# A hybrid trunk layer with a gated delta rule: token-major k, v and norms of q by VectorE's block transposes and copies between partitions

## The chip, the cores and the metric

The kernel runs on one core of one Trainium2 chip. The metric is the device time of one launch, in microseconds (us); the kernel before has a median of 2256.19 us over three runs, from 2256.06 to 2256.45.

A core has five engines that run their own instruction lists side by side: PE (matrix products), ACT (activations), DVE (element-wise work and reductions), POOL (a slower general engine) and SP, which here only issues DMAs. They meet at semaphores. SBUF is the on-chip memory of 128 partitions, PSUM the memory in which PE's products land.

## The reference

One decoder layer on 16 meta tokens and 2048 tokens with 1024 channels, all in float32:

```python
h = rmsnorm(x, norm_g); p = h @ w_in            # 1024 -> 8208 columns
q, k, v = split(silu(causal_dwconv4(p_qkv)))     # 8 heads of 128 channels
q = l2norm(q) * 128**-0.5;  k = l2norm(k)
g = -exp(A_log) * softplus(a + dt_bias);  beta = sigmoid(b)
o = chunk_gated_delta_rule(q, k, v, g, beta)     # state S per head, 128 x 128
#   S_t = a_t (I - beta_t k_t k_t^T) S_{t-1} + beta_t k_t v_t^T,   o_t = S_t^T q_t
o_dn = rmsnorm(o, dn_out_g) * silu(z_A)
o_sc = sc_b * causal_dwconv3(sc_c * sc_h) * silu(sc_z)
x = x + concat(o_dn, o_sc) @ w_out;  return rmsnorm(x, final_g)
```

The delta rule is worked out by chunks. Within a chunk a unit lower triangular matrix I + M is inverted, and from chunk to chunk only S is handed on. The sums of squares that normalize q are taken over a token's 128 channels, and the factor is applied to the output.

## The kernel before

The projection is the bulk of PE's work: 128 jobs, each 128 columns of `w_in` by the tokens of one half (1024 tokens, in three groups; the first half's first group holds the meta tokens too: 272, 384 and 384 tokens, 256 in the second half's first). Weights and activations are split into a high and a low part (`wh`, `wl`, `hh`, `hl`), so a group takes 24 matmuls: `mm<-hh,wh` and `mm<-hl,wh` in turn, then `mm<-hh,wl`. ACT takes a job's first tap of the convolution out of PSUM, DVE adds the other taps (rows `acc`). After both halves comes the output projection.

Beside the projections run four streams for 16 heads, 8 heads on each half, numbered 0 to 15 here. Each is a Python generator.

- `delta_front`: decays `E`, the products of k with k and of q with k, and the inverses of the 32 by 32 diagonal blocks. These are a chain of 31 pairs on DVE, `prod<-nb,XT` and `XT<-prod`. `prod` begins as a pattern copied from the constant `eyep`. Its result goes to `xtd` in DRAM in four copies.
- `delta_back`: four copies bring the blocks back as `W<-xtd`. k, v and q of a head lie channel-major, [channel, token]. PE transposes k (L1138), v (L1147) and q (L1158), 8 tiles of 128 by 128 each, in six batches of four; ACT writes k out of PSUM scaled into `kd`, DVE writes v times `ir` into `vr`, ACT squares q's transposes and accumulates the sums in `ssq`. The blocks are transposed (`X<-W`), and products p1 to p4 (`ta<-X,E` is p1) make the inverse of the whole chunk, in `W`. `qd<-ged` loads the decays, `qd<-qd,q` multiplies q by them.
- `delta_scan`: for each of 8 chunks of 128 tokens a chain over three engines: PE `rec<-S,k`, DVE `yy`, PE `rec<-yy,W`, ACT `vn`, PE `rec<-vn,kd`, DVE `S`; `o<-S,qd` and `o<-vn,P` give the output.
- `delta_out`: norm, gate and store.

The order on PE, ACT, DVE and POOL is what the program issues. Class `Model` (L30 to L107) keeps a planned clock for each engine and each tile; a stream yields the planned time until its next step can run, and between two projection pieces the streams that are due run their next step. A stream that isn't due leaves the place to projection matmuls. Where no projection piece may be issued yet, because a job is waiting for a stream (`require`), the planned clock is moved on and the streams' steps stand one behind the other. Requirements: the job of k of head i needs the scan of head i-2 done, q the blocks of head i-2, v the step ("vr", i-1), the gate's job the output of head i-2. `delta_back` of head i starts when `delta_front` of head i and the scan of head i-1 are through.

All DMAs are issued on SP, in the order in which the program gives them. Each signals on one of eight semaphores, taken in turn, and is issued only when the one eight places ahead has landed.

Of the kernel before, what the change touches and what calls it, by code (L numbers as in the profile page):

```python
# [29 lines left out]
class Model:  # L30
    """Time of each engine and of each tile, as work is issued; it decides the order of issue only."""
# [32 lines left out]
    def after(self, *aps, slot=None, eng=None, lag=0.0, least=0.02):  # L64
        """Time until the tiles are written, the slot is free and the engine is through but for lag."""
# [96 lines left out]
class Recorded:  # L162
    """The engines of a core, with all that they are given entered into the model."""
# [10 lines left out]
def hybrid_trunk(  # L174
# [41 lines left out]
    # ---- order of emission: a stream of projections, cut into pieces, and streams of dependent  # L216
    # steps that are issued between the pieces. `model` follows the engines as they are given work;
    # a step yields the time until what its successor needs is there.
# [28 lines left out]
    def when_done(fn, ap, most=100.0):  # L247
        """Issue fn once ap has been written."""
        timed.append((clk() + min(after(ap), most), fn))
# [46 lines left out]
    def newton(dst, a, y, t):  # L296
        """dst = y (1.5 - 0.5 a y^2): one Newton step for a ** -0.5 from y."""
        nc.vector.tensor_tensor(out=t, in0=y, in1=y, op=ALU.mult)
        nc.vector.scalar_tensor_tensor(t, t, -0.5, a, op0=ALU.mult, op1=ALU.mult)
        nc.vector.scalar_tensor_tensor(dst, t, 1.5, y, op0=ALU.add, op1=ALU.mult)  # L300
# [16 lines left out]
    # ---- constants of the first phase  # L317
# [12 lines left out]
    # eyep[32 q + block, m, i] = (i == 8 q + m)  # L330
    eyep = vt(pp, [128, 8, 32], "eyep")
# [10 lines left out]
    def constants():  # L342
# [29 lines left out]
        nc.gpsimd.memset(eyep, 0.0)  # L372
        for q in range(4):
            for m in range(8):
                nc.gpsimd.memset(eyep[32 * q : 32 * q + 32, m, 8 * q + m : 8 * q + m + 1], 1.0)
# [13 lines left out]
    def turn(hf, xt, k0, i, col, n, g):  # L389
        """Channels 4 k0 .. 4 k0 + 3 of a token tile into h^T."""  # L390
# [18 lines left out]
    def statistics(xt, n, jk):  # L409
        """mean square + eps and its approximate power -0.5."""  # L410
# [6 lines left out]
    def rootmean(xt, n):  # L417
        """(mean square + eps) ** -0.5 by ACT and GpSimd."""
# [14 lines left out]
    def prologue0():  # L433
        """h^T = (RMSNorm(x))^T of the first half as float32r parts hi + lo, [channel, k, token]
        by group."""
# [100 lines left out]
    def normalize(i):  # L536
        """RMSNorm of token tile i of the second half, to DRAM until the first half is through."""
        xt = vt(dp, [128, NC, 128], "kd").rearrange("p c i -> p (c i)")
        nc.sync.dma_start(xt, xs[HALF + 128 * i :][:128])
        yield after(xt)  # L540
        st = statistics(xt, 128, vt(dp, [128, 1840], "gw", dt=BF16))
# [48 lines left out]
    def hold(tag="ta", keep=False):  # L590
        """Wait until no step holds tag over several yields; or hold it."""
# [7 lines left out]
    def gates(hf):  # L599
        """Token-major gate values [128, head, chunk]; on half 0 chunk 8 holds the meta tokens."""  # L600
# [21 lines left out]
        gw = vt(dp, [128, 920], "gw")  # L622
# [24 lines left out]
        # e = exp(-|a|), exp(-|b|), exp(min(b, 0))  # L647
# [11 lines left out]
        # log1p(e) = 2 atanh(s), s = e / (2 + e) <= 1 / 3  # L659
# [35 lines left out]
        G[hf] = dict(beta=beta, gcum=gcum, neg=neg, nch=nch)  # L695
        yield 2.0
        done.add(("G", hf))

    # ---- projections
# [76 lines left out]
    def conv_job(hf, s, col, t, pre, emit):  # L776
        """Projection, causal width-4 convolution and SiLU of channel tile t of q | k | v."""
# [43 lines left out]
    def slot_jobs(hf, s):  # L821
# [51 lines left out]
        # short convolution of channel tile s  # L873
# [67 lines left out]
    # ---- gated delta rule  # L941
    def substitution(nb, XT, prod):
        """Rows of (I + N)^-1 of unit lower triangular 32 x 32 blocks, a block and 8 columns per
        partition; nb[j, i] = N[i, j], XT[col, i], prod[col, i] = identity on entry."""
# [9 lines left out]
    def decay(hf, row0, n, E, gc):  # L954
        """E[j, c, i] = exp(g_i - g_j) for i >= j, else 0."""
# [15 lines left out]
    def delta_front():  # L971
        """Decays, the two triangular matrices, and the inverses of the diagonal blocks."""
# [664 lines left out]
```

## Time and profile before

| | |
|---|---|
| median of three runs | 2256.19 us |
| span of the profiled execution | 2248.0 us |
| lies around it (difference) | 8.2 us |
| PE busy | 2175.4 us, 97% |
| DVE, ACT, POOL busy | 65%, 38%, 7% |

Busy time is the sum over an engine's instructions; what is not busy in the span is a wait. The profiled execution's own time is not recorded apart from its span, so the median stands for it: the two differ by 8.2 us, which are the launch and the end around the first and last instruction. Times in the rows are microseconds from the start of the span. Where a row says `x4`, four like instructions were put together; the start is that of the first.

### The profile page before, as it was taken

The page shows a single profiled execution, that of the slowest core. Times are in us where ns is not written, and L with a number is a line of the kernel's source. Part 1 is how long each engine was busy: PE and PEld are TensorE (multiplying, and loading weights), DVE is VectorE, ACT ScalarE, POOL GpSimd, SP SyncE. Part 2 cuts the span into 40 slices and gives each one's busy share as a digit, 9 for nine tenths or more (in the row PEclk, how much of TensorE's full clock was granted, in tenths as well). Part 3 has the DMA queues.
Part 4 walks back from the last instruction along what each step waited for, and adds up shares of the span by engine and source line. Part 5 has one row for each costly group of instructions (what it writes and reads, how often), then busy time and mean ns, then how long its engine had stood idle before and what let it go on. Part 6 is the DMA issues. An engine that isn't in the chain of part 4 may idle for free.

```text
span 2248.0 us, 38710 instructions
## 1 busy us (share of the span) xinstructions
PE 2175.4 (97%) x15024; PEld 2061.8 (92%) x15024; DVE 1456.6 (65%) x4031; ACT 864.9 (38%) x2080; POOL 153.3 (7%) x312
## 2 busy tenths in 40 slices
PE   6999999999999999999999999999998799999998
PEld 6999999999999998999999999999998798888886
DVE  4676867676767767776868677676766465544322
ACT  5534434444444333443434343525352324422111
POOL 4000100000000000101000000000000000000000
PEclk9999999999999999999999999999999899999999
DMA  6444345443535677524343544253546664645321
GB/s 140 75 81 70 84 68 91 67 93 67 92 67 104 82 83 60 134 43 80 52 83 57 78 52 83 48 88 43 88 49 60 53 94 139 222 164 189 119 94 57
DMA packets 257237, 196.46 MB, mean 87 GB/s; under 512 B 62085, under 2 KB 226446, under 8 KB 257054
## 3 DMA queue, kind: packets, MB, share of 16 engines
q1 hardware_dynamic: 257054, 194.00, 47.5%
q8 instruction: 118, 1.93, 0.4%
q14 instruction: 65, 0.53, 0.1%
HBM read 157.89 MB, written 36.06 MB: 86 GB/s over the span
## 4 chain that ended last, share of the span: by engine, by line
PE 87%; DMA 6%; DVE 4%; SPq 1%; ACT 1%; issue 1%; POOL 0%; POOLq 0%; DVEq 0%; ACTq 0%
PE mm L118 74%; PE ta L118 7%; PE rec L118 4%; PE o L118 2%; SPq L118 1%; DMA nb<-nbd 1%; DMA wr<-in_w_in_dram 1%; DMA kd<-in_x_dram 1%; DVE prod L118 1%; DMA xtd<-XT 1%; DMA W<-xtd 1%; ACT junk L118 1%; DVE acc L118 1%; DVE XT L118 1%; DMA nbd<-E 0%
## 5 line engine op out<-in xcount | busy, mean ns | idle before, releaser
L118 PE MATMUL mm<-hh,wh 128*128 128x384 f32 (+3 forms) x3328 | 1043.6, 335 | 6.4 <-ACT hh L118 5.3
L118 PE MATMUL mm<-hl,wh 128*128 128x384 f32 (+3 forms) x3328 | 1015.1, 326 | 0.0
L118 PEld LDWEIGHTS mm<-hh,wh 128*128 128x128 f32 x3328 | 626.8, 189 | 21.0 <-ACT hh L118 5.9
L118 PEld LDWEIGHTS mm<-hl,wh 128*128 128x128 f32 x3328 | 627.3, 189 | 9.7
L118 PE MATMUL mm<-hh,wl 128*128 128x384 f32 (+3 forms) x3200 | 622.6, 327 | 2.8 <-DVE wl L118 2.8
L118 PEld LDWEIGHTS mm<-hh,wl 128*128 128x128 f32 x3200 | 512.6, 189 | 9.9 <-DVE wl L118 3.2
L118 DVE TENSOR_TENSOR wl<-wr,wh 128x512 fp32r<-128x512 f32 x348 | 233.8, 691 | 98.8 <-ACT wh L118 67.0
L118 DVE SCALAR_TENSOR_TENSOR acc<-raw,pcol,acc 128x384 f32<-128x384 f32 (+2 forms) x432 | 245.5, 573 | 60.5 <-ACT acc L118 55.9
L118 ACT ACTIVATE wh<-wr 128x1024 fp32r<-128x1024 f32 x178 | 187.8, 1055 | 79.3 <-PE mm L118 44.5
L118 DVE SCALAR_TENSOR_TENSOR prod<-nb,XT 128x8 f32<-128x8 f32 (+30 forms) x496 | 192.8, 389 | 39.1 <-DMA nb<-nbd 34.0
L118 DVE TENSOR_REDUCE XT<-prod 128x8 f32<-128x16 f32 (+30 forms) x496 | 147.2, 297 | 17.0
L118 ACT ACTIVATE raw<-mm 128x272 f32<-128x272 f32 (+2 forms) x144 | 65.7, 456 | 214.1 <-PE mm L118 214.1
L118 ACT ACTIVATE vn<-rec,cj 128x128 f32<-128x128 f32 x128 | 46.9, 366 | 252.0 <-PE rec L118 246.7
L118 ACT ACTIVATE sc_c<-mm 128x384 f32<-128x384 f32 (+4 forms) x99 | 45.0, 456 | 161.8 <-PE mm L118 158.0
L118 PE MATMUL mm<-oh,wh 128*128 128x512 f32 x256 | 101.9, 398 | 0.0
L118 PE MATMUL mm<-ol,wh 128*128 128x512 f32 x256 | 100.3, 392 | 0.0
L118 DVE TENSOR_TENSOR y<-mm,y 128x512 f32<-128x512 f32 x23 | 15.9, 692 | 110.7 <-PE mm L118 110.7
L118 DVE SCALAR_TENSOR_TENSOR yy<-rec,neg,vr 128x128 f32<-128x128 f32 x128 | 44.4, 347 | 62.3 <-PE rec L118 61.8
L118 ACT ACTIVATE ojk<-y 128x512 bf16<-128x512 f32 x23 | 14.5, 631 | 182.6 <-DVE y L118 127.0
L118 ACT ACTIVATE acc<-mm,pcol 128x272 f32<-128x272 f32 (+2 forms) x144 | 78.2, 543 | 0.0
L118 DVE SCALAR_TENSOR_TENSOR S<-S,egl,rec 128x128 f32<-128x128 f32 x104 | 35.8, 344 | 59.2 <-PE rec L118 58.3
L118 POOL TENSOR_TENSOR opy<-mo,nhalf 128x4 f32<-128x4 f32 x32 | 35.3, 1102 | 544.0 <-DVE mo L118 507.3
(244 smaller groups left out, 2548.8 us busy)
## 6 DMA issues: line engine op xcount, KB each, us to landing
wr<-in_w_in_dram SPq DMA_DIRECT2D x128, 512.0 KB, 9.0
wr<-mixd SPq DMA_DIRECT2D x50, 512.0 KB, 4.5
E<-gtd SPq DMA_DIRECT2D x16, 512.0 KB, 4.1
qd<-ged SPq DMA_DIRECT2D x16, 512.0 KB, 8.4
nb<-nbd SPq DMA_DIRECT2D x64, 128.0 KB, 5.3
mixd<-zs SPq DMA_DIRECT2D x32, 256.0 KB, 3.2
out_dram<-y SPq DMA_DIRECT2D x16, 512.0 KB, 2.6
mixd<-sc_y SPq DMA_DIRECT2D x32, 192.0 KB, 2.4
```

The source lines that it names most:

```text
L118: r = real(*args, **kw)
```

## The change

For each head, `delta_back` does without PE's 24 transposes and ACT's 8 squares of them.

- k: DVE transposes all 32 by 32 blocks into `tk`, a tile with the place of `qd`; 16 copies (`move_blocks`) then carry blocks between partitions into `kd`, and ACT scales `kd` in place.
- q: DVE transposes blocks into a tile with the place of `gw`, ACT squares it, DVE sums it to `part` (32 sums per partition), and four small products per head with `sel` add the four partition groups and put the sums in token order; DVE copies them to `ssq`.
- v: DVE transposes blocks into the place of `gw`, 16 copies carry them into `vr`, now laid out [block of channels, chunk, channel], and four multiplications by `ir` follow.
- `qd<-ged` is issued after these copies, since it shares its place with `tk`. The step ("vr", i) that the next v job needs is set after v's block transposes.
- `move_blocks` enters its 16 copies into the planner as one DMA of 1.92 us.
- `eyep` goes; `prod` is built on POOL for each head by a memset and four selections. `sel` is made once from the identity. `gates` and `normalize` hold `gw`, and the scan reads `vr` in its new layout.

```diff
-    # eyep[32 q + block, m, i] = (i == 8 q + m)
-    eyep = vt(pp, [128, 8, 32], "eyep")
+
+    sel = vt(pp, [128, 32], "sel")
...
-        nc.gpsimd.memset(eyep, 0.0)
-        for q in range(4):
-            for m in range(8):
-                nc.gpsimd.memset(eyep[32 * q : 32 * q + 32, m, 8 * q + m : 8 * q + m + 1], 1.0)
+        nc.vector.tensor_reduce(
+            out=sel, in_=ident.rearrange("p (a t) -> p t a", t=32), axis=AX.X, op=ALU.add
+        )
...
+        yield from hold("gw")
...
+        yield from hold("gw", True)
+        gw = vt(dp, [128, 1024], "gw")
...
-            nc.gpsimd.tensor_copy(prod, eyep)
+
+            nc.gpsimd.memset(prod, 1.0)
+            for q in range(4):
+                nc.gpsimd.affine_select(
+                    out=prod[32 * q : 32 * q + 32],
+                    in_=prod[32 * q : 32 * q + 32],
+                    pattern=[[-1, 8], [1, 32]],
+                    compare_op=ALU.is_equal,
+                    fill=0.0,
+                    base=-8 * q,
+                    channel_multiplier=0,
+                )
...
+    def turn_blocks(out_, in_):
+
+
+        nc.vector.transpose(
+            out=out_.rearrange("p b c j -> p c b j"), in_=in_.rearrange("p c (b j) -> p c b j", j=32)
+        )
+
+    def move_blocks(whole, out_, in_):
+        for a in range(4):
+            for b in range(4):
+                tc.nc.sync.dma_start(out_[a][32 * b : 32 * b + 32], in_[32 * a : 32 * a + 32, b])
+        model.issue("DMA", 1.92, [whole], [in_])
...
+            kd = vt(dp, [128, NC, 128], "kd")
+            vr = vt(dp, [128, 4, NC, 32], "vr")
+            tk = vt(dp, [128, 4, NC, 32], "qd")
+            turn_blocks(tk, k_)
+            move_blocks(kd, [kd[:, :, 32 * a : 32 * a + 32] for a in range(4)], tk)
+            yield after(eng="DVE", lag=0.3)
+            yield from hold("gw", True)
+            tq = vt(dp, [128, NC * 4, 32], "gw")
+            nc.vector.transpose(out=tq.rearrange("p b j -> p (b j)"), in_=q_.rearrange("p c i -> p (c i)"))
+            yield after(tq)
+            nc.scalar.activation(tq, tq, AF.Square)
+            yield after(tq, eng="DVE", lag=0.3)
+            part = vt(dp, [128, NC, 4], "part")
+            nc.vector.tensor_reduce(
+                out=part.rearrange("p c b -> p (c b)"), in_=tq, axis=AX.X, op=ALU.add
+            )
+            while ("conv", hf, 16 + hd, 2) not in done:
+                yield 0.3
+            yield after(d["vT"], eng="DVE", lag=0.3)
+            tv = vt(dp, [128, 4, NC, 32], "gw")
+            turn_blocks(tv, d["vT"][:, m0 : m0 + 128 * NC].rearrange("p (c i) -> p c i", i=128))
+            done.add(("vr", i))
+            move_blocks(vr, [vr[:, a] for a in range(4)], tv)
+            held.discard("gw")
             qd = vt(dp, [128, NC, 128], "qd")
             nc.sync.dma_start(
                 qd.rearrange("p c i -> p (c i)"),
                 ged[hf, r0 : r0 + NC].rearrange("c i -> (c i)").partition_broadcast(128),
             )
-            kd = vt(dp, [128, NC, 128], "kd")
-            vr = vt(dp, [128, NC, 128], "vr")
-            while ("conv", hf, 16 + hd, 2) not in done:
-                yield 0.3
-            for b4 in range(2):
-                cs = slice(4 * b4, 4 * b4 + 4)
-                yield after(slot=(pta, "ta"), least=0.3)
-                yield from hold()
-                pk = ptile(pta, "ta", [128, 4, 128])
-                for c in range(4):
-                    tr(pk[:, c, :], k_[:, 4 * b4 + c, :])
-                for c in range(4):
-                    cc = 4 * b4 + c
-                    nc.scalar.activation(kd[:, cc], pk[:, c, :], AF.Copy, scale=cd[:, cc : cc + 1])
-                yield after(d["vT"], slot=(pta, "ta"), least=0.3)
-                yield from hold()
-                pv = ptile(pta, "ta", [128, 4, 128])
-                for c in range(4):
-                    c0 = m0 + 128 * (4 * b4 + c)
-                    tr(pv[:, c, :], d["vT"][:, c0 : c0 + 128])
+            yield after(part, slot=(pta, "ta"))
+            yield from hold()
+            pq = ptile(pta, "ta", [128, 512])
+            for b in range(4):
+                mmf(pq[32 * b : 32 * b + 32, 0:NC], lhsT=sel, rhs=part[:, :, b])
+            yield after(pq, kd, eng="DVE", lag=0.3)
+            nc.vector.tensor_copy(ssq, pq[:, 0:NC])
+            for cc in range(NC):
+                nc.scalar.activation(kd[:, cc], kd[:, cc], AF.Copy, scale=cd[:, cc : cc + 1])
+            yield after(vr, eng="DVE", lag=0.3)
+            for a in range(4):
                 nc.vector.tensor_tensor(
-                    out=vr[:, cs],
-                    in0=pv,
-                    in1=ir[:, cs].unsqueeze(2).to_broadcast([128, 4, 128]),
-                    op=ALU.mult,
+                    out=vr[:, a], in0=vr[:, a], in1=ir.unsqueeze(2).to_broadcast([128, NC, 32]), op=ALU.mult
                 )
-                yield after(slot=(pta, "ta"), least=0.3)
-                yield from hold()
-                pq = ptile(pta, "ta", [128, 4, 128])
-                for c in range(4):
-                    tr(pq[:, c, :], q_[:, 4 * b4 + c, :])
-                for c in range(4):
-                    cc = 4 * b4 + c
-                    nc.scalar.activation(junk[:, 0:128], pq[:, c, :], AF.Square, accum_out=ssq[:, cc : cc + 1])
-            done.add(("vr", i))
...
-                        y, pr[:, :128], g_["neg"][:, hd, c : c + 1], vr[:, c, :], op0=ALU.mult, op1=ALU.add
+                        y.rearrange("p (a j) -> p a j", j=32),
+                        pr[:, :128].rearrange("p (a j) -> p a j", j=32),
+                        g_["neg"][:, hd, c : c + 1],
+                        vr[:, :, c, :],
+                        op0=ALU.mult,
+                        op1=ALU.add,
```

The rest of the diff removes comments. What the change does to the order of issue is seen at three places.

First PE, in the scan of head 0, from one chunk to the next; before, with projection matmuls `mm` between the chain's steps:

```order
L118 MATMUL mm<-hh_189,wh 128x272
L118 MATMUL mm<-hl_190,wh 128x272
L118 MATMUL rec<-S,k 128x128
L118 MATMUL o<-S,qd 128x128
L118 MATMUL mm<-hh_189,wh 128x272
L118 MATMUL mm<-hl_190,wh 128x272
L118 MATMUL rec<-ident,os 128x128 x4
L118 MATMUL mm<-hh_189,wh 128x272
L118 MATMUL mm<-hl_190,wh 128x272
L118 MATMUL mm<-hh_189,wh 128x272
L118 MATMUL mm<-hl_190,wh 128x272
L118 MATMUL rec<-yy,W 128x128
```

The same stretch of PE's list now, in the scan's second half:

```order
L118 MATMUL mm<-hh_428,wl 128x384 x4
L118 MATMUL rec<-S,k 128x128
L118 MATMUL o<-S,qd 128x128
L118 MATMUL rec<-yy,W 128x128
L118 MATMUL rec<-vn,kd 128x128
L118 MATMUL o<-vn,P 128x128
L118 MATMUL rec<-S,k 128x128
L118 MATMUL o<-S,qd 128x128
L118 MATMUL rec<-ident,os 128x128 x4
L118 MATMUL rec<-yy,W 128x128
L118 MATMUL rec<-vn,kd 128x128
L118 MATMUL o<-vn,P 128x128
```

The rows of the chain now stand one behind the other without projection matmuls, for four chunks and a third in this scan.

Then DVE near the end of the substitution of head 14 (`prod`, `XT`) where `delta_back` of head 13 stands; before:

```order
L118 SCALAR_TENSOR_TENSOR acc<-raw,pcol,acc 128x256
L118 SCALAR_TENSOR_TENSOR prod<-nb,XT 128x8x31
L118 TENSOR_REDUCE XT<-prod 128x8
L118 SCALAR_TENSOR_TENSOR acc<-raw,pcol,acc 128x256 x2
L118 SCALAR_TENSOR_TENSOR acc<-raw,pcol,acc 128x384
L118 TENSOR_TENSOR E<-E,gcum_11366 128x1024
L118 TENSOR_TENSOR vr<-ta,ir 128x512
L118 SCALAR_TENSOR_TENSOR acc<-raw,pcol,acc 128x384 x2
L118 TENSOR_TENSOR vr<-ta,ir 128x512
L118 SCALAR_TENSOR_TENSOR acc<-raw,pcol,acc 128x384
L118 STREAM_TRANSPOSE X<-W 32x8x32 x3
```

DVE at this place now:

```order
L118 SCALAR_TENSOR_TENSOR prod<-nb,XT 128x8x30
L118 TENSOR_REDUCE XT<-prod 128x8
L118 SCALAR_TENSOR_TENSOR prod<-nb,XT 128x8x31
L118 TENSOR_REDUCE XT<-prod 128x8
L118 STREAM_TRANSPOSE qd<-k 128x8x4x32
L118 TENSOR_TENSOR E<-E,gcum_11439 128x1024
L118 STREAM_TRANSPOSE gw<-q 128x1024
L118 COPY cd<-E 128x8
L118 TENSOR_REDUCE part<-gw 128x32
L118 TENSOR_TENSOR nb<-k,nb 128x2x128
L118 TENSOR_TENSOR nb<-q,nb 128x2x128
L118 STREAM_TRANSPOSE gw<-vT 128x8x4x32
```

The transposes of k, q and v and the sum `part` of head 13 stand behind the last pairs of the substitution of head 14; on PE the four products that read `part` stand here:

```order
L118 MATMUL mm<-hh_10760,wl 128x384 x8
L118 MATMUL mm<-hh_10350,wh 128x256
L118 MATMUL mm<-hl_10351,wh 128x256
L118 MATMUL mm<-hh_10350,wh 128x256
L118 MATMUL mm<-hl_10351,wh 128x256
L118 MATMUL mm<-hh_10350,wh 128x256
L118 MATMUL mm<-hl_10351,wh 128x256
L118 MATMUL ta<-part,sel 32x8 x4
L118 MATMUL mm<-hh_10350,wh 128x256
```

Ahead of the products with `sel` are six matmuls of 256 columns and the end of a group of 384 columns, whose `acc` rows stand on DVE at the pair `prod<-nb,XT 128x8x24`.

Last SP, around the blocks of head 2; before:

```order
L118 DMA qd<-ged 128x1024
L118 DMA kd<-in_x_dram 128x1024
L118 DMA wr<-in_w_in_dram 128x8x128
L118 DMA Q<-in_norm_g_dram 128x512
L118 DMA mixd<-zs 128x4x128
L118 DMA xnd<-kd 128x1024
L118 DMA wr<-in_w_in_dram 128x8x128 x3
L118 DMA xtd<-XT 32x8x32 x4
L118 DMA W<-xtd 32x8x32 x4
L118 DMA E<-gtd 128x1024
```

SP around the blocks of head 2 now:

```order
L118 DMA xtd<-XT 32x8x32 x4
L1131 DMA kd<-qd 32x8x32
L118 DMA W<-xtd 32x8x32 x4
L1131 DMA kd<-qd 32x8x32 x15
L1131 DMA vr<-gw 32x256 x16
L118 DMA qd<-ged 128x1024
L118 DMA wr<-in_w_in_dram 128x8x128 x2
L118 DMA E<-gtd 128x1024
L118 DMA mixd<-sc_y 128x2x128
```

The load of `qd` stood ahead of the copies of `xtd` and now stands behind 32 copies between partitions, and so do the weight loads `wr` and `E<-gtd` that follow.

## Rows read from the trace of the kernel before

**Rows 1.** Page, busy us of each engine, share of the span, instructions.

```profile
PE 2175.4 (97%) x15024; PEld 2061.8 (92%) x15024; DVE 1456.6 (65%) x4031; ACT 864.9 (38%) x2080; POOL 153.3 (7%) x312
```

**Rows 2.** Page, chain that ended last, share of the span by engine.

```profile
PE 87%; DMA 6%; DVE 4%; SPq 1%; ACT 1%; issue 1%; POOL 0%; POOLq 0%; DVEq 0%; ACTq 0%
```

**Rows 3.** PE by tile shape: busy us, mean ns; idle before them and releaser.

```profile
L118 PE MATMUL ta<-ident,k 128*128 128x128 f32 x128 | 19.2, 272 | 1.6 <-DVE vr L118 1.6
L118 PE MATMUL ta<-X,E 32*32 32x32 f32 x512 | 12.3, 197 | 17.6 <-issue 13.6 <-DVE X L118 3.8
```

**Rows 4.** Timeline of PE, head 4: start us, us, what.

```profile
631.22 0.60 PE L118 MATMUL ta<-ident,k 128*128 128x128 f32 x4
631.58 0.42 PE L118 MATMUL mm<-hh,wh 128*128 128x384 f32 x1
631.84 0.34 PE L118 MATMUL mm<-hl,wh 128*128 128x384 f32 x1
632.01 0.49 PE L118 MATMUL ta<-ident,vT 128*128 128x128 f32 x3
```

**Rows 5.** Timeline of four engines in a scan: handoffs between them.

```profile
802.73 0.34 DVE L118 SCALAR_TENSOR_TENSOR S<-S,egl,rec 128x128 f32<-128x128 f32 x1
...
803.12 0.49 PE L118 MATMUL rec<-S,k 128*128 128x128 f32 x2 [2.25 <-DVE S L118]
...
805.09 0.38 PE L118 MATMUL rec<-yy,W 128*128 128x128 f32 x2
...
805.51 0.37 ACT L118 ACTIVATE vn<-rec,cj 128x128 f32<-128x128 f32 x1 [5.62 <-PE rec L118]
...
1918.66 0.34 DVE L118 SCALAR_TENSOR_TENSOR yy<-rec,neg,vr 128x128 f32<-128x128 f32 x1
...
1922.97 0.39 PE L118 MATMUL rec<-S,k 128*128 128x128 f32 x2
...
1923.19 0.39 PE L118 MATMUL o<-S,qd 128*128 128x128 f32 x2
...
1923.39 0.35 DVE L118 SCALAR_TENSOR_TENSOR yy<-rec,neg,vr 128x128 f32<-128x128 f32 x1 [1.49 <-PE rec L118]
```

**Rows 6.** DVE by tile shape.

```profile
L118 DVE TENSOR_TENSOR wl<-wr,wh 128x512 fp32r<-128x512 f32 x348 | 233.8, 691 | 98.8 <-ACT wh L118 67.0 <-PE mm L118 31.5
L118 DVE SCALAR_TENSOR_TENSOR acc<-raw,pcol,acc 128x384 f32<-128x384 f32 x288 | 175.8, 616 | 44.6 <-ACT acc L118 41.5
...
L118 DVE STREAM_TRANSPOSE X<-W 32x256 f32<-32x256 f32 x48 | 20.7, 432 | 21.9 <-DMA W<-xtd 20.9
L118 DVE TENSOR_TENSOR qd<-qd,q 128x1024 f32<-128x1024 f32 x16 | 19.6, 1226 | 0.5
...
L118 DVE SCALAR_TENSOR_TENSOR prod<-nb,XT 128x224 f32<-128x224 f32 x16 | 9.0, 566 | 0.2
...
L118 DVE TENSOR_REDUCE XT<-prod 128x8 f32<-128x232 f32 x16 | 6.4, 397 | 0.5
```

**Rows 7.** ACT by tile shape.

```profile
L118 ACT ACT_TABLE_LOAD x43 | 55.2, 1283 | 5.2 <-DVE gw L118 3.7 <-PEq L1621 0.8
...
L118 ACT ACTIVATE E<-E 128x1024 f32<-128x1024 f32 x16 | 17.0, 1060 | 0.7 <-POOL E L118 0.5
```

**Rows 8.** Timeline of SP, head 4: time from start of first issue to last.

```profile
626.97 2.73 SPq L118 DMA_DIRECT2D xtd<-XT  x4
633.85 1.79 SPq L118 DMA_DIRECT2D W<-xtd  x4
```

**Rows 9.** The tile `xtd`, its copies in and out, over the whole span.

```profile
DMA to landing us min/median/max: 1.6/2.7/13.0
```

**Rows 10.** Page, DMA issues: count, KB each, median us to landing.

```profile
qd<-ged SPq DMA_DIRECT2D x16, 512.0 KB, 8.4
nb<-nbd SPq DMA_DIRECT2D x64, 128.0 KB, 5.3
```

**Rows 11.** Busy us of engines in a stretch, granted clock, DMA share, GB/s.

```profile
1740.00:1760.00 20.00, 19.63 (x130) 19.11 (x128) 11.12 (x22) 12.10 (x34) 1.23 (x2) 1.00 0.90 71
1760.00:1780.00 20.00, 6.61 (x102) 5.97 (x103) 4.87 (x11) 2.29 (x5) 0.00 (x0) 0.66 0.60 55
```

More of the change, by code (lines that the diff above doesn't have):

```diff
@@ L621, in gates @@
         pt = ptile(pta, "ta", [128, 512])
-        gw = vt(dp, [128, 920], "gw")
+        yield from hold("gw", True)
+        gw = vt(dp, [128, 1024], "gw")
         ab2 = gw[:, 0:288].rearrange("p (c m) -> p c m", m=32)
@@ L1121, in delta_back @@
                 )
+            kd = vt(dp, [128, NC, 128], "kd")
[21 more added lines that the diff above has]
+            move_blocks(vr, [vr[:, a] for a in range(4)], tv)
+            held.discard("gw")
             qd = vt(dp, [128, NC, 128], "qd")
```

## The prediction

> **What bounds the kernel now.** The page's busy line comes first: PE works 97% of the span, DVE 65%, ACT 38%, POOL 7% [rows 1]. The chain of waits agrees: 87% of it lies on PE, 6% on DMA, 4% on DVE [rows 2]. So nearly every microsecond of work taken off PE shortens the span, and every wait put on PE lengthens it, as long as no other work of PE can be drawn into the gap; PE's list is fixed, so it can't. The third view is PE by tile shape: the transposes of k are 128 matmuls of 272 ns, and the first product on the blocks, `ta<-X,E`, is where PE already waits, 17.6 us in all, of which 13.6 is one wait [rows 3]. That wait lies at head 14, in a stretch in which PE is busy 6.61 of 20 us, DMA 60%, and the granted clock falls to 0.66 [rows 11], towards the lower of its two levels (1.2 of 2.4 GHz). A matmul's own duration overlaps with its neighbours', so costs of PE are read start to start from a timeline [rows 4]; what a step in a dependent chain costs is read from the handoffs between engines [rows 5].
>
> **What PE is spared.** Six batches of four transposes for each of 16 heads, 96 batches. A batch occupies 631.22 to 631.58, 0.36 us; the next matmul then takes 0.26 instead of 0.17 (631.58, 631.84, 632.01) [rows 4]. With that 0.09 a batch costs 0.45, or 43; without it 35. Some batches follow each other directly and pay the break once: I take 40. Added are 64 small products with `sel`, each two matmuls as the products of `ta<-X,E` (512 matmuls for 256 of them): 128 times 12.3 / 512 us [rows 3] is 3.1, and 16 breaks of 0.09 are 1.4: 5 with rounding, 3 to 6. PE's work falls by 35 (29 to 40).
>
> **What moves: the scans.** The planner had filled the gaps of a scan's chain with projection matmuls, and the transposes had been some of the filling. Now the next k job waits for a scan at six places, and the chain's rows stand bare. By my count of PE's list 13 2/3 chunks are bare: 4 1/3 of head 0, 1 1/3 of head 2, 1 each of heads 3 and 4, 4 of head 6, 2 of head 7; before, none. DVE to PE takes 802.73 to 803.12, 0.39; PE to ACT 805.09 to 805.51, 0.42; PE to DVE 1922.97 to 1923.39, 0.42 [rows 5]. A chunk has three of PE's starts and three of the others', 2.4 us, of which PE's own five products (0.22 from `rec<-S,k` to the next [rows 5], less for the others) are about 1.0. Idle is thus at least 1.4 a chunk. At most it is a chunk as long as now with filling, 1918.66 to 1923.39, 4.73, less 1.0: 3.7. DVE is busy 65%, and a step of the chain may find a `wl` or `acc` of 0.6 to 0.7 [rows 6] ahead: two such steps at 0.65 times about half of 0.65 add 0.4, ACT and the slots the rest. I take 2.2: 30 us (19 to 51).
>
> **A wait at head 13.** The four products with `sel` stand on PE six matmuls, about 0.7 us, after the group whose `acc` rows stand on DVE at the pair of 24. DVE has ahead of `part`: four `acc` at 0.616, eight pairs of the substitution at 0.566 + 0.397, two `wl` at 0.691 [rows 6], that is 11.6; a transpose of k, bounded by 1.23 (another 1024-wide operation) and four times 0.432 [rows 6], and the subtraction in E, 1.23; then the transpose of q, the square on ACT behind a table load and the exponential (1.28 + 1.06 + 1.06 [rows 7]) and `part`, another 1.2. In all about 20, of which some has run by then: PE waits 17 (10 to 22). Behind `ta<-part,sel` all of PE's projections are queued, so ACT and DVE run dry as well. A smaller wait of this kind at head 14 is priced at 4 (0 to 8).
>
> **The copies.** SP issues four copies of 32 partitions in 1.79 us, 0.45 each [rows 8]; 16 take 7.2. They land after 1.6 at least, 2.7 in the median, up to 13.0 [rows 9]. The copies of k have the whole step of q to land. Those of v decide: DVE's multiplications of `vr` stand ahead of `X<-W`, so p1 on PE waits for them. From the `sel` products to p1 PE has about 10.8 us of rows in most heads (7.7 to 14.3). Against this stand: the end of v's transpose 0.8 after `sel`, 7.2, 2.7, a DVE operation in front 0.69, the last multiplication 0.43 and three transposes 1.3 [rows 6], a handoff 0.39: 13.5, or 2.7 late, 43 over 16 heads. The waits of now at `ta<-X,E`, 17.6 [rows 3], go, because X stands later: 26. `qd<-ged`, 8.4 to landing [rows 10], was loaded ahead and now comes behind all copies; DVE's `egl` stands just behind X and stalls the merging. I add 4: 30. The lower end is -17, copies never late. The upper: a burst of four has been 6.88 from its first issue to the reader's issue, 626.97 to 633.85, of which issuing takes 2.73 [rows 8]; 4.2 more a head gives 6.9 times 16 less 17, 93.
>
> The row has a median of 2.7 us for copies of 32 KB and 5.3 for `nb<-nbd` of 128 KB [rows 9, 10]: half the time for a quarter of the bytes. The Trainium skill, "DMA: Bandwidth & Descriptors", section "Bandwidth", says that transfers under 64 KB are dominated by their descriptors and asks for batching. By that rule 32 more copies a head, in pieces of 128 bytes or 1 KB, would come out as the second rival below; by the row they cost the 30 above. The trace agrees with the rule's direction.
>
> **The clock.** After the wait of 13.6 the granted clock is 0.66 in its stretch [rows 11]. A wait of 17 would cost some 3 behind it, the smaller ones 2: 5 (0 to 15).
>
> **What is hidden.** DVE gains per head three transposes and a sum of 1024 columns (each about 1.23 [rows 6], 4.9) and 0.4 for four multiplications instead of two: some 85 us, DVE then 69% busy, not the bound. ACT loses 128 squares. Building `prod` on POOL, five operations for one copy, runs while `nb<-nbd` lands (5.3 [rows 10]); if that cover went, the substitution would start some microseconds later, and `delta_back` with it.
>
> **Sum.** -35 + 30 + 17 + 4 + 30 + 5 = +51 on the span of 2248.0: 2299; with the 8.2 around it 2307, which stands to the median of 2256.19. The bounds together reach from -28 to +160.
>
> **The rivals.**
>
> 1. Faster, 2227 to 2235. Waits don't appear: the copies land near 1.6, PE's 10.8 us cover them and the waits at `ta<-X,E` go (-17), the bare chunks cost 1.4 (19), head 13's wait is 10, no clock is lost. -40 or -35 + 19 + 10 - 17 is -28 or -23, plus 2256. For it: PE is at 97%, and the lowest landings; against it: the `sel` wait is in the lists whatever the copies do.
>
> 2. A storm of copies, 2360 to 2414, far slower. Only eight DMAs can be out at once. If eight land in 8.4, as a load of `qd` does [rows 10], 16 copies take 16.8 in place of 9.9, and p1 is 9.6 late: 154 less 17 is 137 in place of 30, 2414; with half the heads so, 2360. `wr` loads behind them come late next, and PE waits for `wl`. For it: the landing of 13.0 [rows 9] and a DMA share of 0.90 ahead of the wait [rows 11]; against it: the median of 2.7. It decides from a landing of about 4 us for eight on. The rule of the Trainium skill quoted above speaks for it.
>
> 3. About as before, 2256 to 2261. The bare chunks cost their least (19), the copies nothing in sum, no clock: -40 or -35 + 19 + 17 + 4 is 0 or +5. For it: each is within its bounds; against it: all three must be small while head 13's wait is full.
>
> **How the numbers follow.** Forecast 0.61, faster 0.14, storm 0.18, about as before 0.07. The forecast's own range is 2270 to 2350. The range for 8 in 10 reaches below to 2240, which leaves out most of the faster case, and above to 2395, which leaves out half of the storm. A change of 0.2%, 4.5 us, is what a measurement of this kernel can tell from none: faster by more 0.14, within 0.06, slower by more 0.80 (the rest of the third rival goes to slower).
>
> **What would show it.** PE's busy sum falls by about 35 while its idle grows by some 85. Waits on DVE `S`, `yy` and ACT `vn` at PE's `rec` rows sit at the ends of the scans of heads 0, 2, 3, 4, 6 and 7, about 2.2 a chunk; one of over 10 at `ta<-part,sel` of head 13. DVE waits for the DMAs `vr<-gw` and `qd<-ged`, PE for X behind it. The granted clock dips there. The forecast is wrong if PE's idle stays near 73 us (then faster or unchanged), if copies from `gw` land after 4 us and more (storm), or if the waits stand elsewhere.

## The result and the profile after

The changed kernel takes 2483.1 us (median of four runs, 2474.5 to 2486.8) against 2256.1: 1.100 times the time before, 95% interval 1.098 to 1.102. The forecast was 2307, its range ended at 2395: slower was right, the size was not.

The page of the changed kernel first: busy us of each engine, and the chain of waits by engine and by line.

```profile
PE 2238.0 (90%) x14768; PEld 2100.8 (85%) x14768; DVE 1540.7 (62%) x4156; ACT 844.3 (34%) x1846; POOL 184.5 (7%) x343
...
PE 66%; SPq 12%; DMA 10%; DVE 7%; issue 3%; ACT 2%; POOL 0%; DVEq 0%; POOLq 0%; ACTq 0%
PE mm L118 55%; SPq L1131 9%; PE ta L118 4%; PE rec L118 4%; DMA wr<-in_w_in_dram 4%; SPq L118 3%; PE o L118 2%; DVE prod L118 1%; DMA xtd<-XT 1%; DVE wl L118 1%; DMA vr<-gw 1%; DMA nb<-nbd 1%; DVE XT L118 1%; DVE sc_y L118 1%; DMA sc_c<-xnd 1%
```

PE has 256 matmuls fewer than in [rows 1], as counted, and yet is busy 62.6 us longer; its idle time (span less busy) grows by 174.4, from 72.6 to 247.0. The two make the 237 us of the spans. In [rows 2] PE had 87% of the chain; now 12% of it is SP's queue, and 9% of the span is the one line that issues the copies between partitions, L1131.

What the wait consists of, by the view of waits (us in total, times, longest), for PE, DVE and ACT:

```profile
PE ta L118 <- DVE X L118: 46.2, 23, 13.1
PE mm L118 <- DVE wl L118: 22.6, 13, 7.6
PE ta L118 <- DVE part L118: 22.1, 2, 17.5
PE ta L118 <- ACT nb L118: 21.7, 6, 10.6
PE mm L118 <- ACT wh L118: 21.5, 3, 11.0
PE rec L118 <- DVE S L118: 14.6, 8, 6.8
...
PE rec L118 <- ACT vn L118: 11.1, 13, 2.4
...
PE rec L118 <- DVE yy L118: 6.2, 8, 1.8
...
DVE vr L118 <- DMA vr<-gw: 88.6, 44, 8.4
...
ACT kd L118 <- DMA kd<-qd: 126.2, 13, 19.5
```

The same view of the kernel before, for PE:

```profile
PE rec L118 <- DVE S L118: 7.4, 3, 3.5
...
PE ta L118 <- DVE X L118: 3.8, 2, 3.2
...
PE mm L118 <- DVE wl L118: 2.8, 2, 1.7
...
PE mm L118 <- ACT wh L118: 1.1, 1, 1.1
```

PE's wait for X, 3.8 before, beside one of 13.6 for which the profile names no releaser [rows 3], is 46.2 and comes 23 times. Its waits for `wl`, for ACT's `nb` and for `wh` together grow from 3.9 to 65.8. DVE stands still in front of `vr` and ACT in front of `kd`, 215 us together, and what they would have done next (X, `wh`, `nb`, `wl`) is what PE waits for.

SP's timeline around head 2 shows why (start, time from the first issue to the end of the last):

```profile
434.96 5.45 SPq L118 DMA_DIRECT2D xtd<-XT  x4
440.51 0.64 SPq L1131 DMA_DIRECT2D kd<-qd  x1
444.10 1.78 SPq L118 DMA_DIRECT2D W<-xtd  x4
445.93 10.56 SPq L1131 DMA_DIRECT2D kd<-qd  x15
456.58 10.06 SPq L1131 DMA_DIRECT2D vr<-gw  x16
466.69 0.58 SPq L118 DMA_DIRECT2D qd<-ged  x1
467.38 1.02 SPq L118 DMA_DIRECT2D wr<-in_w_in_dram  x2
```

SP issues without a pause from 445.93 to 466.64: some 0.66 us a copy from one issue to the next, not the 0.45 that the prediction took from `W` [rows 8]. The copies of v stand behind those of k. On the same stretch DVE and ACT:

```profile
452.18 1.24 DVE L118 STREAM_TRANSPOSE gw<-vT 128x1024 f32<-128x1024 f32 x1
...
468.16 0.43 DVE L118 TENSOR_TENSOR vr<-vr,ir 128x256 f32<-128x256 f32 x1 [2.25 <-DMA vr<-gw]
468.50 1.36 DVE L118 STREAM_TRANSPOSE X<-W 32x256 f32<-32x256 f32 x3
```

```profile
458.13 2.45 ACT L118 ACTIVATE kd<-kd,cd 128x128 f32<-128x128 f32 x8 [9.62 <-DMA kd<-qd]
460.49 1.04 ACT L118 ACTIVATE wh<-wr 128x1024 fp32r<-128x1024 f32 x1
```

v's blocks are transposed by 453.4; X can follow only at 468.5, 15 us later. ACT stands still for 9.6 us and only then splits the next weights into `wh`. PE itself waits for X less than 1 us in this head, after two waits of about 1 us for `nb`. Its longest wait for X is at head 5, where v's copies are issued until 838.8:

```profile
828.64 10.17 SPq L1131 DMA_DIRECT2D vr<-gw  x16
```

```profile
841.09 1.12 PE L118 MATMUL ta<-X,E 32*32 32x32 f32 x22 [13.06 <-DVE X L118]
```

The copies themselves are quick: landing, min/median/max, of all DMAs of the tiles `kd` and `vr`, and the page's rows of the copies (KB each, median):

```profile
DMA to landing us min/median/max: 1.9/2.0/9.3
```

```profile
DMA to landing us min/median/max: 1.8/1.9/16.0
```

```profile
kd<-qd SPq DMA_DIRECT2D x256, 32.0 KB, 2.0
vr<-gw SPq DMA_DIRECT2D x256, 32.0 KB, 1.9
```

The 16.0 belongs to a load at the start, `vr<-in_x_dram`; of the 320 landings of copies that the trace has, 11 took over 4 us.

Last the clock, by stretches (length, busy us of PE, PEld, DVE, ACT, POOL, granted clock, DMA share, GB/s): the bare chunks of head 0, and a stretch with waits near head 6.

```profile
264.00:280.00 16.00, 11.55 (x40) 8.83 (x40) 13.37 (x73) 2.98 (x12) 1.92 (x2) 0.55 0.23 51
...
975.00:995.00 20.00, 12.56 (x125) 10.56 (x125) 8.60 (x21) 2.83 (x7) 0.00 (x0) 0.59 0.69 162
```

Both, 0.55 and 0.59 of full speed, lie near the lower of the two levels; the second follows a wait of 11.0 us for `wh` that ended at 974.1. Over the whole run the mean granted clock falls from 0.991 to 0.939.

### The profile page after: what moved, and what is told of

Same layout as the page of the kernel before. It is cut to its first block, busy times and chain, and to the rows that moved or that the text cites. A ratio compares the mean times of both kernels' runs of the same rounds, so it can differ in the third digit from the quotient of the medians.

```text
span 2485.0 us, 38941 instructions
## 1 busy us (share of the span) xinstructions
PE 2238.0 (90%) x14768; PEld 2100.8 (85%) x14768; DVE 1540.7 (62%) x4156; ACT 844.3 (34%) x1846; POOL 184.5 (7%) x343
## 4 chain that ended last, share of the span: by engine, by line
PE 66%; SPq 12%; DMA 10%; DVE 7%; issue 3%; ACT 2%; POOL 0%; DVEq 0%; POOLq 0%; ACTq 0%
PE mm L118 55%; SPq L1131 9%; PE ta L118 4%; PE rec L118 4%; DMA wr<-in_w_in_dram 4%; SPq L118 3%; PE o L118 2%; DVE prod L118 1%; DMA xtd<-XT 1%; DVE wl L118 1%; DMA vr<-gw 1%; DMA nb<-nbd 1%; DVE XT L118 1%; DVE sc_y L118 1%; DMA sc_c<-xnd 1%
## 5 line engine op out<-in xcount | busy, mean ns | idle before, releaser
L118 PE MATMUL mm<-hh,wh 128*128 128x384 f32 (+3 forms) x3328 | 1064.2, 341 | 34.7 <-ACT wh L118 21.5
L118 PE MATMUL mm<-hl,wh 128*128 128x384 f32 (+3 forms) x3328 | 1035.2, 332 | 1.8 <-DVE hl L118 1.8
L118 PEld LDWEIGHTS mm<-hh,wh 128*128 128x128 f32 x3328 | 645.6, 195 | 52.4 <-ACT wh L118 22.4
L118 PEld LDWEIGHTS mm<-hl,wh 128*128 128x128 f32 x3328 | 646.1, 195 | 12.5 <-DVE hl L118 2.6
L118 PEld LDWEIGHTS mm<-hh,wl 128*128 128x128 f32 x3200 | 524.4, 193 | 33.7 <-DVE wl L118 27.4
L118 PE MATMUL ta<-nb 128*128 128x256 f32 x384 | 67.9, 316 | 26.6 <-ACT nb L118 21.7
L118 PEld LDWEIGHTS ta<-X,E 32*32 32x32 f32 (+1 forms) x768 | 34.6, 141 | 64.1 <-issue 43.1
L118 PE MATMUL ta<-X,E 32*32 32x32 f32 (+1 forms) x768 | 40.4, 229 | 52.7 <-DVE X L118 46.2
L118 PEld LDWEIGHTS ta<-nb 128*128 128x128 f32 x384 | 62.2, 220 | 30.2 <-ACT nb L118 23.7
L118 ACT ACTIVATE kd<-kd,cd 128x128 f32<-128x128 f32 x128 | 39.2, 388 | 135.0 <-DMA kd<-qd 126.2
```

The lines of the kernel that those rows point to most:

```text
L118: r = real(*args, **kw)
```

## Experiments

Theory A: the 32 issues on SP make the loss, since engines stand in front of the copies' data and other DMAs stand behind the copies. Theory B: the new order of issue on the engines makes it. "One copy" below stands for `e1_one_copy` throughout. Ratios are to the kernel before as it ran beside each experiment (medians of 2253.5 to 2256.8), with their 95% intervals.

**How many issues.** Three kernels with PE's list of the changed kernel, row by row; only `move_blocks` differs.

```diff
 # e1_one_copy; out_, in_ are the whole tiles, straight
-        for a in range(4):
-            for b in range(4):
-                tc.nc.sync.dma_start(out_[a][32 * b : 32 * b + 32], in_[32 * a : 32 * a + 32, b])
+        tc.nc.sync.dma_start(out_, in_)
 # e1b_four
+        for a in range(4):
+            tc.nc.sync.dma_start(out_[a], in_[:, a])
 # e2_halves: each of the 16 copies in two, chunks 4 * h .. 4 * h + 3
```

> The 16 copies of k and the 16 of v per head become one straight copy each (2 issues in place of 32, the same bytes; blocks stay on their partitions, so kd and vr hold the wrong tokens). PE's list is the same row by row. Theory A (issue: SP needs 0.6 us per copy, kd and vr come late, ACT and DVE stand in front of them, PE's clock falls with PE's waits): 2483 falls to 2270 to 2320, waits at ACT kd (126 us) and DVE vr (89 us) shrink to under 30 each. Theory B (order: bare chunks and the wait at the sel products, and the clock behind these, make the loss): stays above 2420.

> Four straight copies for k and four for v (8 issues a head in place of 32, wrong tokens); PE's list is that of the changed kernel. Theory A, cost by issues: between one copy each (2305) and 16 each (2483), near 2310 to 2340 since eight issues take some 5 us. If the number hardly matters up to 16 and something else in the full kernel does the damage: as 2483.

> Each copy is cut into two of half the bytes: 64 issues per head. PE's list is the same. Theory A: some 16 us more of issuing per head on the path, 16 heads, 2650 to 2780. Theory B: within 30 us of 2483.

Measured: 2304.7 us (ratio 1.021, 1.016 to 1.026), 2326.0 (1.032, 1.029 to 1.035) and 2827.1 (one run, so without an interval). So 2, 8, 32 and 64 issues a head make 2305, 2326, 2483 and 2827, the first two within theory A's figures and the last beyond them. The first six added cost 0.22 us each (21 over 6 times 16), the next 24 0.41, the last 32 0.67, a little more than the 0.6 us for which one keeps SP busy. Only the first step also cuts the rows that a copy moves, from 4 KB to 128 bytes (k) and 1 KB (v); from 8 to 32 issues they stay as they are. For the 178 us between one copy and the changed kernel this is theory A. The waits that theory A names mostly go with one copy, while those for `part` and of the `rec` rows stay:

```profile
ACT kd L118 <- DMA kd<-qd: 22.8, 5, 9.0
PE ta L118 <- DVE part L118: 22.2, 2, 17.6
...
PE rec L118 <- DVE S L118: 13.8, 7, 6.1
...
PE rec L118 <- ACT vn L118: 10.7, 13, 2.4
...
PE rec L118 <- DVE yy L118: 6.2, 7, 1.8
...
DVE vr L118 <- DMA vr<-gw: 3.9, 3, 2.5
...
PE ta L118 <- DVE X L118: 1.2, 2, 1.0
```

The busy lines of one copy and of the halves, and the halves' chain:

```profile
PE 2176.2 (95%) x14768; PEld 2051.4 (89%) x14768; DVE 1534.7 (67%) x4156; ACT 845.7 (37%) x1846; POOL 183.4 (8%) x343
```

```profile
PE 2272.2 (80%) x14768; PEld 2131.7 (75%) x14768; DVE 1541.4 (55%) x4156; ACT 844.4 (30%) x1846; POOL 184.5 (7%) x343
...
PE 57%; SPq 23%; DMA 8%; DVE 7%; issue 3%; ACT 2%; POOL 0%; DVEq 0%; POOLq 0%; ACTq 0%
PE mm L118 47%; SPq L1132 20%; PE ta L118 4%; PE rec L118 4%; DMA wr<-in_w_in_dram 3%; SPq L118 3%; PE o L118 2%; DMA xtd<-XT 1%; DVE prod L118 1%; DVE wl L118 1%; DMA vr<-gw 1%; DVE XT L118 1%; DMA sc_c<-xnd 1%; DVE sc_y L118 1%; DMA nb<-nbd 1%
```

The copies' line has 20% of the halves' chain. And the same 14768 matmuls take 2176, 2238 and 2272 us at mean clocks of 0.973, 0.939 and 0.881: PE's waits are paid twice, as idle and as slower work behind.

**Whose data somebody stands in front of.** `e11_k_q` and `e16_v_q` have 16 copies a head each; v and k respectively stay on PE, and the norms of q run in a stream of their own, as in `e10_q_late` (below, no copies, 2274).

```diff
 # e11_k_q, on e10_q_late: k; kd scaled in the stream of the norms, planner told 9.6
+            tk = vt(dp, [128, 4, NC, 32], "gw")
+            turn_blocks(tk, k_)
+            move_blocks(kd, [kd[:, :, 32 * a : 32 * a + 32] for a in range(4)], tk)
 # e16_v_q, on e10_q_late: v; multiplications of vr ahead of X, planner told 1.92
+            tv = vt(dp, [128, 4, NC, 32], "gw")
+            turn_blocks(tv, d["vT"][:, m0 : m0 + 128 * NC].rearrange("p (c i) -> p c i", i=128))
+            move_blocks(vr, [vr[:, a] for a in range(4)], tv)
+            yield after(vr, eng="DVE", lag=0.3)
```

> As e10_q_late, and k goes by VectorE and 16 copies, scaled late, the planner told 9.6 us; v stays on PE, so no copy stands ahead of the blocks' transposes. Theory A (copies cost where someone stands in front of them, v's above all): 2235 to 2270. Rival (16 copies on SP cost their 9.6 us a head wherever they stand, by the loads behind them): 2330 to 2400.

> The counterpart of e11_k_q: v goes by VectorE and 16 copies with the multiplications of vr ahead of X as in the changed kernel (planner told 1.92), k stays on PE, norms of q in a stream of their own. The same number of copies as e11_k_q (2284). If their place decides (16 issues at 0.6 and a landing stand between v and X, some 12 us a head against 10.8 us of PE's rows): 2320 to 2390, PE's wait for X over 40 us. If only their number decides: 2270 to 2300.

Measured: 2284.3 (1.013, 1.010 to 1.017), 14 above theory A's figure, and 2377.8 (1.054, 1.050 to 1.059), within it. Each does without 32 more of PE's batches than `e10_q_late`; even so 16 copies end 10 us above it where nothing of the blocks stands behind them, and 103 above it where X does. The 93 between the two are not the place alone: the second was planned with 1.92 us for the copies and the first with 9.6, which is worth 70 us in `e3_cost` below, and no run separates the two. PE's wait for X differs by 58 of them. The waits of PE for X in the two, and DVE's in the second:

```profile
PE ta L118 <- DVE X L118: 11.6, 6, 5.3
```

```profile
PE ta L118 <- DVE X L118: 69.2, 27, 18.7
...
DVE vr L118 <- DMA vr<-gw: 109.8, 48, 16.1
```

**What stands behind on SP.** 32 copies a head that nobody reads, in the kernel before.

```diff
 # e14_unread
+            for n in range(32):
+                a, b = divmod(n % 16, 4)
+                tc.nc.sync.dma_start(mvd[i % 2, n], k_[32 * a : 32 * a + 32, :, 32 * b : 32 * b + 32])
```

> The kernel before with 32 more copies a head of k's blocks to a scratch in DRAM that nobody reads (some go ahead of xtd in SP's list). Same PE list. If the harm is in those who stand in front of the copies' data: within 25 us of 2256. If the harm is in SP's queue, by the loads and W copies that stand behind 32 issues: 2350 or more.

Measured: 2283.2 (1.013, 1.006 to 1.020), a little above the first figure. The DMAs behind the copies cost some 30 us (13 to 46 by the interval), far less than the 178 between one copy and the changed kernel. Each of these copies kept SP 0.61 us, as in the changed kernel, but some stand earlier on SP, so the 30 are a guide and not the exact share.

**Other ways around the copies.**

```diff
 # e7_late_kd: the eight ACT scalings of kd behind DVE's four multiplications of vr
 # e4_kpool: k's copies issued by POOL
-                tc.nc.sync.dma_start(...)
+                tc.nc.gpsimd.dma_start(...)
 # e3_cost
-        model.issue("DMA", 1.92, [whole], [in_])
+        model.issue("DMA", 9.6, [whole], [in_])
 # e8_late_pool: the three together
 # e5_dram: 1 store to DRAM and 4 loads each for k and v, qd loaded behind
 # e15_blocks_first: moves as in e5_dram; qd early, X and p1 to p4 not behind vr;
 #   kd's scalings, vr's multiplications and the norms of q in a stream of their own
```

> ACT's eight scalings of kd stand behind DVE's multiplications of vr, no longer ahead of them; copies as before. If ACT standing in front of kd is what makes its nb and wh late for PE (126 us of ACT's waits): 2410 to 2450, PE's waits on ACT nb and wh (43 us) go. If SP alone decides (vr's copies come last anyway): within 20 us of 2483.

> The 16 copies of k are issued by POOL, those of v stay on SP; PE's list is the same. Theory A (SP's queue): v's copies and the weight loads no longer stand behind k's, some 10 us a head earlier: 2370 to 2430. Rival C (the copies are slow by themselves, whoever issues them: POOL's issue is no quicker than SP's and kd lands as late): 2460 to 2500.

> The planner is told 9.6 us for 16 copies in place of 1.92; the same 32 copies. It now leaves room for them in PE's order (16.7 bare chunks in place of 10). Theory A (SP's issuing is the bound and it stays): at most half of the loss comes back, 2380 to 2470. Theory B (the order is at fault, the planner's price of the copies decides): 2300 or less.

> All three together: k's copies on POOL, kd scaled late, the planner told 9.6 us a move. Theory A: below each of the three, 2300 to 2380, still above 2256 because of the bare chunks. Theory B: about as the planner's price alone.

> Blocks move by DRAM: one store of the whole tile and four loads, for k and for v, 10 issues per head in place of 32; qd is loaded after kd is scaled. Theory A: 2320 to 2400 (6 us of issuing, but two landings in a row of 2 to 4 us each per tile). Theory B: above 2420, with some 14 bare chunks in the order in place of 10.

> The whole change in another order: qd loaded early, blocks moved by DRAM (one store and four loads each for k and v), X and p1 to p4 not behind them, and scaling kd, multiplying vr and the norms of q in a stream of their own. If the harm is in who stands in front of the copies' data: 2260 to 2310, at or below one copy each with wrong tokens (2305), well below 2407 of the same moves with X behind vr. If the number of moves decides: about 2400.

`e7_late_kd`: 2495.0 (1.108, 1.103 to 1.113), no gain, as its second figure had it. ACT's wait for `kd<-qd` falls from 126.2 to 23.3, but PE's for X rises from 46.2 to 115.6: v's copies come last in any case, and ACT's wait had run beside theirs. `e4_kpool`: 2499.9 (1.110, 1.105 to 1.115), no gain either: against theory A's figure, and at the edge of rival C's. POOL's issues are indeed hardly quicker, but `kd` isn't as late: ACT's wait for it falls to 16.7. DVE's wait for `vr` fell only to 66.1, and PE now waits 83.9 us for `part`; the view of POOL at head 2 has the reason:

```profile
441.86 9.31 POOL L1132 DMA_DIRECT2D kd<-qd  x16 [31.28 <-PE mm L118]
451.17 1.11 POOL L118 TENSOR_SCALAR_AFFINE_SELECT E<-E 128x1024 f32<-128x1024 f32 x1
```

The selection on E of the next head stands behind 16 issues of 0.58 us; ACT's exponential of E and, behind it, the square of q wait for it. The row that waits has changed, the price has not. `e3_cost`: 2413.1 (1.071, 1.065 to 1.078), within A's figure: told the truth, the planner gets 70 us back. `e8_late_pool`: 2452.7 (1.089, 1.085 to 1.094), worse than the planner's price alone; neither theory had it. `e5_dram`: 2406.7 (1.066, 1.058 to 1.074), just above A's figure. `e15_blocks_first`: 2352.3 (1.044, 1.042 to 1.046), better than `e5_dram` by 54 with the same moves, yet above its figure. It moves X ahead, but also `qd`, `kd`'s scalings and the norms of q, so the 54 are the new order as a whole and not the place of X alone.

**What remains with one copy.** 49 us, with 2 issues a head and, by the prediction's count, 35 us less work on PE.

```diff
 # e9_one_copy_late_sel: on one copy, the sel products and ssq behind p4
 # e12_no_dve: on one copy, DVE's three transposes left out, readers take k, vT and q
 # e13_quarter: the kernel before; of each batch of four transposes the first only
-                for c in range(4):
-                    tr(pk[:, c, :], k_[:, 4 * b4 + c, :])
+                tr(pk[:, 0, :], k_[:, 4 * b4, :])
```

> As e1_one_copy (one straight copy for k and one for v, wrong tokens in kd and vr), and the four products with sel and the copy to ssq stand behind p4, at the end of delta_back. If the wait at the sel products (22 us of PE's waits in e1_one_copy, 2 places) is what remains with its clock: 2305 falls to 2270 to 2285. If the waits in front of the scans' rows decide the rest: within 10 us of 2305.

> As e1_one_copy (one straight copy for k and one for v, wrong tokens), and VectorE's three transposes a head are left out too (copies and ACT's square read k, vT and q themselves); PE's list is the same, the planner still counts the transposes. If DVE's added work is why PE waits at head 13 and at the scans' rows (the wait at the sel products only moved to other rows in e9): 2305 falls to 2265 to 2285, the wait of 17.6 at the sel products to under 12. If the bare order decides: within 10 us of 2305.

> The kernel before with one of each batch's four transposes; its readers take that one four times (wrong values). PE's list is else the same row by row. What PE's time is worth with nothing else changed: 18 of 24 transposes a head at 0.09 us are 26 us, 2256 falls to 2225 to 2235 if PE's time is the span; to 2240 to 2256 if the gain turns into waits for ACT, DVE or DMAs that are late anyway.

`e9`: 2324.2 (1.032, 1.027 to 1.036), a miss. The wait at the products with `sel` is gone, and one nearly as long stands at the next reader, six matmuls further on in the same job. One copy and `e9`, PE's timeline:

```profile
1702.69 0.29 PE L118 MATMUL ta<-part,sel 128*32 128x8 f32 x8 [17.59 <-DVE part L118]
```

```profile
1710.91 0.58 PE L118 MATMUL ta<-nb 128*128 128x256 f32 x1 [15.70 <-ACT nb L118]
```

In one copy's stretch 1685 to 1705 DVE is busy 17.09 of 20 us and PE 2.41: what DVE has queued there makes the wait, whichever row meets it. `e12`: 2295.6 (1.019, 1.014 to 1.023), at the edge of "the order decides": DVE's transposes are worth at most some 9 us (the intervals of the two ratios overlap), and the wait at `part` stays 16.4. `e13`: 2241.4 (0.994, 0.993 to 0.996): of the 26 us reckoned only 12 to 15 reach the end, as the lesser of the two figures has it. In the profiled execution PE's busy time falls by 14.1 (2175.4 to 2161.3) and its idle time grows by 10.8, so a part of the 26 was never there and a part turns into waits; the shares are not settled.

With one copy PE is busy as long as before, though it has 256 matmuls fewer (2176.2 against 2175.4), and idle for 126.7 us instead of 72.6. Of these 54.1 more, the waits for `part` (22.2, before none) and those of the `rec` rows for `S`, `vn` and `yy` (30.7, before 7.4) are 45.5, most of it at rows that the new order has moved or laid bare. That speaks for the new order as the cause of most of the 49, but no run had the new steps in the old order, so this is not shown.

**Versions.**

```diff
 # e6_q_only: k, v by PE, norms of q by DVE and sel ahead of them, no copies
 # e10_q_late: the same, the norms in a stream of their own behind
```

> Only the norms of q go by VectorE and the sel products; k and v by PE's transposes, vr in its old layout, qd loaded early: no copies between partitions. Theory A: within 15 us of 2256, faster by about 10 if nothing else is late (32 of 96 batches at 0.45 us less 5). Theory B: the wait at the sel products stays, 2270 or more.

> k and v by PE's transposes as before, norms of q by VectorE, ACT and sel in a stream of their own behind them, so that ACT scales kd first. No copies between partitions. If the wait of PE for ACT's kd (18.8 us in e6_q_only) was the square standing in front: 2240 to 2252, faster than before by the 32 batches at 0.45 us less 5 for sel. If the order shifts waits elsewhere: 2256 to 2270.

Measured: 2264.9 (1.003, 1.001 to 1.006) and 2274.4 (1.010, 1.007 to 1.012). The first is within A's 15 us, but not the 10 faster; the second lies above both its figures: the wait for `kd` is gone, and waits for `os` on DVE (22.4 us, before 10.5) have come. None of the versions that compute everything beats the kernel before.

## Why the prediction was wrong

- **PE's work, -35.** The count of matmuls was right, their worth was not: PE's busy sum, said to fall by about 35, rose by 62.6. With the copies' waits nearly gone it is what it was (one copy), and in `e13_quarter` about half of such a gain reached the end.
- **Bare chunks, +30.** Right in place, too high in price. The waits of PE's `rec` rows for `S`, `vn` and `yy` are 14.6 + 11.1 + 6.2 = 31.9, but 12.9 of them stand at four `rec<-S,k` rows outside the bare chunks; in the chunks themselves they are 19.0, the least that the prediction allowed. In the trace 34 handoffs have no projection matmul between them, 11 1/3 chunks; the prediction and the section on the change counted also the first row of each run, which still follows projection matmuls. What the step left out is that the chunk's own matmuls run near the lower level there: two of `rec<-S,k` in head 0 are 3.99 us apart, not 3.2.

```profile
272.40 0.79 PE L118 MATMUL rec<-S,k 128*128 128x128 f32 x2
...
276.39 0.79 PE L118 MATMUL rec<-S,k 128*128 128x128 f32 x2
```

- **Heads 13 and 14, +17 and +4.** 22.1 in two waits, 17.5 and 4.6. The best of the terms, and its reason, DVE's list, holds as far as it was tried: without the products at this place the wait stood at the next reader (`e9`), and without DVE's transposes 16.4 of it stayed (`e12`).
- **The copies, +30.** The step that failed. It said that SP issues one in 0.45 us, that "the copies of k have the whole step of q to land", and that those of v need 7.2 us of issuing. Issues are 0.66 apart; in 15 of 16 heads the last copy of k is issued only after v's transposes have ended, and v's copies stand behind it. In head 2 X starts 15.1 us after the end of v's transposes where 11.0 were reckoned (7.2, 2.7, 0.69, 0.43), over all heads 16.4 in the median, and with one copy 7.7. The step looked for the price at X alone: it has 43 us of lateness there, and PE's wait for X is 46.2. That this is near is partly luck, since X came later than reckoned, and PE, as in head 2 after its waits for `nb`, can come later too. What it put at nothing is the rest: taking 30 of the 32 issues away gives 178 us back (182 in the profiled spans), 120 of idle and 62 of slower work, and of the 120 only 45 are waits for X; another 47 are waits for `wl`, `nb` and `wh`. The upper bound, 93, was drawn from bursts of four. It also adds the burst's 4.2 us to a sum that already holds a landing of 2.7; without that it would have been about 50.
- **ACT and DVE as bystanders.** "What is hidden" looked at their busy shares. An engine that stands in front of late data holds back what its list has next: ACT's `wh` at 460.49 comes after 9.62 us in front of `kd`. So `wh`, `wl` and `nb` came late, of which the prediction named only `wl`, and only in the storm. To take ACT alone out of the way gained nothing (`e7_late_kd`).
- **The clock, +5.** It was priced by one long wait. 62 us more of PE's busy time separate the changed kernel from one copy on the same list.
- **The storm** (2360 to 2414) came nearest, and still 69 us short, with the wrong mechanism: it asked for late landings and eight DMAs out at once. The copies landed in 1.9 to 2.0; at 0.66 from issue to issue that is, by estimate, some three out at a time. The price lay in issuing them. The Trainium skill's rule that the rival leaned on ("DMA: Bandwidth & Descriptors", section "Bandwidth"), that transfers under 64 KB are dominated by their descriptors, pointed the right way, to fewer and larger copies. The section takes the rule from loads out of HBM, and these copies stay in SBUF; no run here shows its reason, and a copy cut to half its bytes (`e2_halves`) kept SP as long as a whole one, 0.59 to 0.60 us.

## What to carry to other kernels

Count the DMAs that a step adds, multiply by the spacing of issues in the trace, put the whole burst into the queue's order, and ask which in-order engine waits for its last piece and what stands behind that instruction. Cover that carried four copies doesn't carry 32: 0.22 us per copy at first, 0.67 at the end. Price their lateness at every reader behind the waiting engines, not only at the one in view. And when a wait lands on the engine that bounds the kernel, its price in this kernel was half as much again, by the clock (62 us of slower work on 120 of idle).

## What the runs showed of the hardware

A copy of 32 KB between partitions keeps SP 0.59 to 0.61 us (medians of `vr` and `kd`); its halves of 16 KB take 0.59 to 0.60, and on POOL the 32 KB take 0.58. The copies to and from `xtd`, 32 KB each as well, take 0.45 in the kernel before, but the copies of 32 KB to DRAM in `e14_unread` 0.61. So neither the bytes nor DRAM as the destination sets the price by itself; what does was not tried. One straight copy of 512 KB is issued in 0.47 and lands in 3.2 (v) and 4.7 (k). DVE's block transposes of 1024 columns take 1.24 us, close to the lower of the two bounds used (1.23).
